# Reading the Toeplitz tiles of an S5 scan back in longer runs

## The chip, the core and the metric

The kernel runs on one core of a Trainium2 chip. The metric is the device time of one execution in microseconds (us). Three executions of the kernel before gave a median of 572.31 us (570.33 to 572.6).

A core has five engines with their own instruction streams: TensorE (PE, matrix products; PEld is its weight load), VectorE (DVE), ScalarE (ACT), GpSimd (POOL) and SyncE (SP), which here issues nearly all transfers (DMAs). Each engine works strictly in its own order. Between engines only semaphores order the work: an instruction names semaphores with a value, and it and everything behind it on its engine stand still until these are reached.

## The reference

One decoder layer on x (1024 tokens by 1024), then a final RMSNorm. Cut to what matters here:

```python
h = rms_norm(x, gain) * (1 + scl) + shift        # adaLN from cond = silu(c)
u, z_ssm, qd, kd, vd, z_diff, qs, ks, vs, z_swa = split_cols(h @ w_in)
y_ssm  = s5_mixer(u, ...)          * silu(z_ssm)   # 16 groups of 16 channels, 64 complex states each
y_diff = diff_attention(qd, kd, vd, ...) * silu(z_diff)            # 4 heads, full causal
y_swa  = sliding_window_attention(qs, ks, vs, ...) * silu(z_swa)   # 4 query heads, window 128
out = rms_norm(x + gate * (concat(y_ssm, y_diff, y_swa) @ w_out), final_gain)
```

Inside `s5_mixer` a diagonal complex recurrence runs over the 1024 tokens. Its output per group is y = Re(C s) + D u, then a GELU and a gated linear unit.

## The kernel before, in words

**The scan in blocks of eight.** The 1024 tokens are cut into 128 blocks of 8. Within a block the output of a group depends on the block's own eight inputs through a 128 by 128 lower block-Toeplitz matrix (8 by 8 lags of 16 by 16), and on the state that comes in from the blocks before. `ssm_lags` builds the lag matrices K (16 rows, per group 8 lags of 16 columns) with small products (`pK`), adds D at lag 0 on VectorE, writes K to the scratch `kscr[m]` in device memory (m is one of two halves of the 16 groups, 8 groups each; every group has 7 lags of zeros ahead of its 8 lags, 15 x 16 elements), and reads the Toeplitz matrix back: partition (s, h) of group a gets the 128 elements that begin s lags into that group's run. That is tile `T` (lines 664 to 684). `ssm_state(m)` makes the states (`pV` products, then `tg` and `Xs` on VectorE), `ssm_out(q)` for q = 0 to 3 does the products `pY` = T u + CA Xs into a bank of PSUM, the GELU in tile `gw`, and stores to the scratch `yscr` (lines 1104 to 1140). `ssm_glu` finishes later.

**Around it.** The S5 work stands between the projections, in this order on TensorE: the key tile `ks`, the query tiles `qs0` and `qs1` of the window attention (`p_ks`, `p_qs`), the gate `z0` (`p_z`), then values `v0` (`p_v`, 256 columns wide, weights in two halves), `q0`, `k0`. A projection's weights are loaded by SP (`wr_...`), split on ScalarE into a high part (`wh_...`) and on GpSimd or VectorE into a low part (`wl_...`), and multiplied with h (`hh`, `hl`) in three products. `next_w` (line 966) issues the load two projections ahead and the split one ahead. The results are copied out of PSUM by ScalarE and VectorE: `ev_q` (line 1174) writes `qs0m`, `qs1m` (two tiles each, both engines), `ev_silu` writes `z`, with a tanh on ScalarE and a product on VectorE.

**What sets the order.** A planner (`Model`, `Mixer`) with its own costs picks, while the program is written, which generator gets to add its next piece. The order on each engine is fixed after that.

**The pages.** Every large tile is one of 50 pages of 128 x 4096 bytes: `page()` (line 249) asks a pool with the one tag `pg` and `bufs=NPG`, where `NPG = 50` (line 240). All 50 are taken long before the S5 block, so a new tile takes over the page of an old one, and its first writer must wait for the last readers and writers of the old one. No line of the kernel says which old tile that is: the pool decides it while the program is built, in the order of the page() calls and of the releases. The planner does not know of it either.

**SP's semaphores.** SP's transfers use eight completion semaphores in turn. A transfer waits for the one eight before it.

**Names in the trace.** All operations have line L109, since one helper records them all, so tiles are told apart by name. The profile leaves out buffer numbers: `wl_v` is either half of the low part.

Of the kernel before, what the change touches and what calls it, by code (L numbers as in the profile page):

```python
# [24 lines left out]
def dap(t, offset, dims):  # L25
    return bass.AP(tensor=t.tensor, offset=t.offset + offset, ap=[list(d) for d in dims])
# [203 lines left out]
def body(ctx, tc, x, c, norm_gain, ada_w, ada_b, w_in, w_out, lam_re, lam_im, log_step,  # L230
# [13 lines left out]
    PE, SP = Eng(mdl, "PE", nc.tensor), Eng(mdl, "SP", nc.sync)  # L244
# [4 lines left out]
    def page(name, shape=(128, 1024), dt=F32):  # L249
        return big.tile(list(shape), dt, name=name, tag="pg", bufs=NPG)  # L250

    def pst(tag, name, shape=(128, 512)):
        t = psum.tile(list(shape), F32, name=name, tag=tag, bufs=BUFS[tag])
        mdl.slot(tag, BUFS[tag], t.tensor.name)
        if tag != "pp":
            held.add(t.tensor.name)
        return t

    def rel(*ts):

        for t in ts:
            held.discard(t.tensor.name)

    def bank(tag, n=1):

        def f():
            ring = mdl.ring.get(tag, [])
            if len(ring) + n <= BUFS[tag]:
                return 0.0
            olds = ring[:n - (BUFS[tag] - len(ring))]  # L270
            if any(o in held for o in olds):
                return 1e9
            return max(max(mdl.w.get(o, 0.0), mdl.r.get(o, 0.0)) for o in olds)
        return f

    def when(cond):
        return lambda: 0.0 if cond() else 1e9

    def tts(o, a, b, op, eng=None):
        (eng or V).tensor_tensor(o, a, b, op)  # L280
# [79 lines left out]
    X = []  # L360
# [67 lines left out]
    PW = {}  # L428
# [192 lines left out]
    kscr = [dram.tile([16, 8, 15, 16], F32, name=f"kscr{m}") for m in range(2)]  # L621

    def ssm_lags():
        kz = page("kz", (16, 8, 7, 16))
        G.memset(kz, 0.0)
        for m in range(2):
            SP.dma_start(kscr[m][:, :, 0:7, :], kz)
        yield (Cn, bank("pt"))
        psc = pst("pt", "psc", (128, 2, 128))
        for u in range(2):  # L630
            PE.transpose(psc[:, u], Cn[:, u], ident)
        A.activation(prm[:, 3], psc.rearrange("p a b -> p (a b)"), AF.Copy)
        rel(psc)
        AP = PW["AP"]

        CA = [[page(f"CA{m}{g2}", (128, 4, 9, 16)) for g2 in range(2)] for m in range(2)]
        PW["CA"] = CA
        u0, u1 = page("ca0", (128, 4, 9, 16)), page("ca1", (128, 4, 9, 16))
        v3 = lambda t, r: t[r].rearrange("p a b c -> p (a b c)")
        for m in range(2):  # L640
            yield ("V",)
            sl = slice(4 * m, 4 * m + 4)
            a4 = [AP[:, u, sl][:, :, :, None].to_broadcast([128, 4, 9, 16]) for u in range(2)]
            c4 = [CT[:, u, sl][:, :, None, :].to_broadcast([128, 4, 9, 16]) for u in range(2)]
            tts(u0, a4[0], c4[0], OP.mult)
            tts(u1, a4[1], c4[1], OP.mult)
            yield ("V",)
            for g2, r in enumerate(RH):
                tts(v3(CA[m][g2], RH[0]), v3(u0, r), v3(u1, r), OP.subtract)
            yield ("V",)  # L650
            tts(u0, a4[0], c4[1], OP.mult)
            tts(u1, a4[1], c4[0], OP.mult)
            yield ("V",)
            for g2, r in enumerate(RH):
                V.scalar_tensor_tensor(v3(CA[m][g2], RH[1]), v3(u0, r), -1.0, v3(u1, r),
                                       op0=OP.mult, op1=OP.subtract)

        yield (dn, bank("pt"))
        dT = cst.tile([16, 16], F32, name="dT")
        pd = pst("pt", "pd", (16, 16))  # L660
        PE.transpose(pd, dn, ident[:16, :16])
        A.activation(dT, pd, AF.Copy)
        rel(pd)
        Tm = [page(f"T{m}", (128, 8, 8, 16)) for m in range(2)]
        for m in range(2):
            K = page(f"K{m}", (16, 8, 8, 16))
            for g2 in range(2):
                yield (CA[m][g2], BS, bank("pt"))
                p = pst("pt", "pK", (16, 4, 128))
                for a in range(4):  # L670
                    PE.matmul(p[:, a], lhsT=BS[:, 4 * m + a, g2],
                              rhs=CA[m][g2][:, a, 0:8, :].rearrange("p a b -> p (a b)"), start=True, stop=True)
                A.activation(K.rearrange("p (a g) b c -> p g a (b c)", g=2)[:, g2], p, AF.Copy)
                rel(p)
            yield (K,)
            dd = sml.tile([16, 8, 16], F32, name="dd", bufs=1)
            tts(dd, ident[:16, None, :16].to_broadcast([16, 8, 16]),
                dT[:, 8 * m:8 * m + 8, None].to_broadcast([16, 8, 16]), OP.mult)
            tts(K[:, :, 0, :], K[:, :, 0, :], dd, OP.add)

            SP.dma_start(kscr[m][:, :, 7:15, :], K)
            SP.dma_start(Tm[m].rearrange("p a b c -> p a (b c)"),
                         dap(kscr[m], 0, [[16, 8], [15 * 128, 16], [15 * 16, 8], [1, 128]]))
        PW["T"] = Tm


# [345 lines left out]
    SM = {"st": 0, "y": 0}  # L1032
# [71 lines left out]
    def ssm_out(q):  # L1104

        m, g2 = divmod(q, 2)
        c0 = math.sqrt(2.0 / math.pi)
        yield (when(lambda: ("x", m) in SM and "T" in PW),)
        yield (SM["X"][m], PW["T"][m], bank("ps"))
        CA, Tm, Uu, Xs = PW["CA"], PW["T"], SM["U"], SM["X"][m]  # L1110
        p = pst("ps", "pY", (128, 4, 128))
        for a in range(4):
            pr = 4 * m + a
            g = 2 * pr + g2
            PE.matmul(p[:, a], lhsT=Tm[m][:, g % 8].rearrange("p a b -> p (a b)"), rhs=Uu[m][:, g % 8],
                      start=True, stop=False)
            PE.matmul(p[:, a], lhsT=CA[m][g2][:, a, 1:9, :].rearrange("p a b -> p (a b)"), rhs=Xs[:, g2, a],
                      start=False, stop=True)
        yield (p, "A")
        w = page("gw", (128, 2, 4, 128))  # L1120
        A.activation(w[:, 0], p, AF.Square)
        yield (w, "V")
        V.tensor_scalar(w[:, 0], w[:, 0], 0.044715, 1.0, op0=OP.mult, op1=OP.add)
        tts(w[:, 0], w[:, 0], p, OP.mult)
        yield (w, "A")
        A.activation(w[:, 0], w[:, 0], AF.Tanh, scale=c0)
        yield (w, "V")
        V.scalar_tensor_tensor(w[:, 1], w[:, 0], 1.0, p, op0=OP.add, op1=OP.mult)
        rel(p)
        for tt in range(8):  # L1130
            SP.dma_start(dap(yscr, (m * 8 + g2) * 16 * 1024 + tt * 128, [[1024, 16], [32 * 1024, 4], [1, 128]]),
                         w[tt * 16:(tt + 1) * 16, 1])
        SM["y"] += 1
        if SM["y"] == 4:
            GW = page("gw", (128, 2, 256))
            YG = [page(f"yg{f}", (128, 8, 128)) for f in range(2)]
            for f in range(2):
                SP.dma_start(GW[:, f], dap(glu_w, f * 128 * 256, [[256, 128], [1, 256]]))
                SP.dma_start(YG[f].rearrange("p a b -> p (a b)"), yscr[f * 128:(f + 1) * 128, :])
            PW["glu"] = (GW, YG)  # L1140
# [33 lines left out]
    def ev_q(name):  # L1174

        q = [page(f"{name}m{m}", dt=F32R) for m in range(2)]

        def f(p, n):
            cs_ = slice(n * 512, (n + 1) * 512)
            hi(q[0], R0, p, R0, cs_)  # L1180
            hi(q[1], R1, p, R1, cs_)
            lo(q[0], R1, p, R0, q[0], R0, cs_)
            lo(q[1], R0, p, R1, q[1], R1, cs_)
        return q, f

    def ev_k(name, m4=True):

        k = [page(f"{name}m{m}", dt=F32R) for m in range(4 if m4 else 3)]

        def f(p, n):  # L1190
            cs_ = slice(n * 512, (n + 1) * 512)
            hi(k[0], R0, p, R0, cs_)
            hi(k[1], R1, p, R1, cs_)
            lo(k[2], R0, p, R0, k[0], R0, cs_)
            lo(k[-1], R1, p, R1, k[1], R1, cs_)
            for m in range(4 if m4 else 2):
                src, dst = (R0, R1)[m % 2], (R1, R0)[m % 2]
                (acopy if name == "ks" else DUP[m])(k[m][dst, cs_], k[m][src, cs_])
        return k, f
# [318 lines left out]
    d_k, f = ev_k("ks")  # L1518
    proj(f)
    d_q = []  # L1520
    for a in range(2):
        q_, f = ev_q(f"qs{a}")
# [6 lines left out]
    for t in ORDER:  # L1529
# [6 lines left out]
        else:  # L1536
            z_ = page(t)
            f = ev_silu(z_)
# [82 lines left out]
    while live or opened < len(parts):  # L1621
# [7 lines left out]
        f, e = mix.first()  # L1629
# [3 lines left out]
        i, n, c, k = u  # L1633
# [35 lines left out]
```

## Time and profile before

| | |
|---|---|
| median of three runs | 572.31 us |
| the profiled execution: its own time | 574.51 us |
| its span, first to last instruction | 572.7 us |
| granted TensorE clock | 0.991 |
| busy: PE, DVE, ACT, POOL | 553.5, 407.0, 262.5, 188.2 us |
| the two reads of `T` | 512 KB each, issued at 135.80 and 143.52 us |
| packets of all transfers | 60634, 57.12 MB |

The profiled execution's own time is 1.8 us more than its span, and 2.2 us above the median of the runs. Times inside the span are given in us from its start. In the rows of a timeline the columns are start, duration, engine, line, operation, output tile <- input tiles, shapes and count of what was merged; in brackets stands how long the engine was idle before and which work ended that. A matmul's duration is modelled, and matmuls overlap: successive starts are 0.23 us apart for a 512-column product.

### The profile page before, as it was taken

The page shows a single profiled execution, that of the slowest core. Times are in us where ns is not written, and L with a number is a line of the kernel's source. Part 1 is how long each engine was busy: PE and PEld are TensorE (multiplying, and loading weights), DVE is VectorE, ACT ScalarE, POOL GpSimd, SP SyncE. Part 2 cuts the span into 40 slices and gives each one's busy share as a digit, 9 for nine tenths or more (in the row PEclk, how much of TensorE's full clock was granted, in tenths as well). Part 3 has the DMA queues.
Part 4 walks back from the last instruction along what each step waited for, and adds up shares of the span by engine and source line. Part 5 has one row for each costly group of instructions (what it writes and reads, how often), then busy time and mean ns, then how long its engine had stood idle before and what let it go on. Part 6 is the DMA issues. An engine that isn't in the chain of part 4 may idle for free.

```text
span 572.7 us, 9240 instructions
## 1 busy us (share of the span) xinstructions
PE 553.5 (97%) x3170; PEld 463.7 (81%) x3170; DVE 407.0 (71%) x1061; ACT 262.5 (46%) x595; POOL 188.2 (33%) x339
## 2 busy tenths in 40 slices
PE   8999999999997999999999999999999999799995
PEld 6667888888887996777788889998888888688884
DVE  3885996997687656778666777744877877666434
ACT  5445221255142545435555766535558545533111
POOL 3354270000135036442646172323332912210011
PEclk9999999999999999999999999999999999899998
DMA  8994076002711430437320111015025604014211
GB/s 287 354 351 94 3 187 153 0 2 47 148 37 47 77 117 38 178 127 226 106 73 2 38 37 38 2 37 158 28 83 170 189 1 129 1 74 147 94 38 73
DMA packets 60634, 57.12 MB, mean 100 GB/s; under 512 B 11375, under 2 KB 52906, under 8 KB 60586
## 3 DMA queue, kind: packets, MB, share of 16 engines
q1 hardware_dynamic: 60518, 56.50, 33.1%
q8 instruction: 25, 0.41, 0.3%
q14 instruction: 23, 0.19, 0.1%
q10 hardware_dynamic: 68, 0.02, 0.0%
HBM read 46.83 MB, written 9.68 MB: 99 GB/s over the span
## 4 chain that ended last, share of the span: by engine, by line
PE 76%; DVE 11%; DMA 5%; ACT 3%; issue 2%; POOL 1%; SPq 1%; POOLq 0%; DVEq 0%
PE po L109 13%; PE pb L109 8%; PE p_v L109 7%; PE p_k L109 6%; PE p_z L109 6%; PE pdO L109 6%; PE p_q L109 5%; PE pS L109 5%; PE p_zs L109 4%; DVE tg L109 3%; PE pdT L109 3%; DMA x<-in_x_dram 2%; PE p_vs L109 2%; PE p_zu L109 2%; PE pa L109 2%
## 5 line engine op out<-in xcount | busy, mean ns | idle before, releaser
L109 ACT ACTIVATE sp<-sp,dmx 128x128 f32<-128x128 f32 (+7 forms) x64 | 49.0, 768 | 16.5 <-DVE dmx L109 15.4
L109 PE MATMUL po<-woh,yh 128*128 128x512 f32 (+1 forms) x136 | 52.5, 386 | 1.1 <-ACT yh L109 1.1
L109 PE MATMUL po<-wol,yh 128*128 128x512 f32 (+1 forms) x136 | 51.6, 379 | 0.5 <-POOL wol L109 0.5
L109 PE MATMUL po<-woh,yl 128*128 128x512 f32 (+1 forms) x136 | 51.4, 378 | 0.0
L109 POOL TENSOR_SCALAR dmx<-dmx 128x1 f32<-128x1 f32 x32 | 8.2, 255 | 111.3 <-ACT oo L109 110.5
L109 DVE CUSTOM_DVE_ANT_0 sp<-pS,bd 128x384 f32<-128x384 f32 (+3 forms) x64 | 33.6, 552 | 10.7 <-PE pS L109 10.5
L109 PE MATMUL p_v<-wh_v,hh 128*128 128x256 f32 x128 | 37.8, 295 | 0.0
L109 PE MATMUL p_v<-wl_v,hh 128*128 128x256 f32 x128 | 36.4, 284 | 1.0 <-POOL wl_v L109 1.0
L109 PE MATMUL p_v<-wh_v,hl 128*128 128x256 f32 x128 | 36.2, 283 | 0.0
L109 POOL TENSOR_TENSOR swp<-swp,swm 128x256 f32<-128x256 f32 x30 | 20.4, 712 | 41.0 <-DVE swm L109 31.9
L109 ACT ACTIVATE jk<-res 128x512 f32<-128x512 f32 (+1 forms) x16 | 9.9, 616 | 46.5 <-DVE res L109 46.5
L109 PEld LDWEIGHTS po<-woh,yh 128*128 128x128 f32 x136 | 25.8, 189 | 5.9 <-ACT yh L109 1.5
L109 PEld LDWEIGHTS po<-wol,yh 128*128 128x128 f32 x136 | 25.8, 190 | 5.2 <-POOL wol L109 1.0
L109 PEld LDWEIGHTS po<-woh,yl 128*128 128x128 f32 x136 | 25.7, 189 | 4.8
L109 PE MATMUL p_k<-hh,wh_k 128*128 128x512 f32 x64 | 26.4, 413 | 0.0
L109 POOL TENSOR_TENSOR wl_z<-wr_z,wh_z 128x256 fp32r<-128x256 f32 x16 | 11.6, 755 | 44.5 <-ACT wh_z L109 44.5
L109 PE MATMUL p_q<-hh,wh_q 128*128 128x512 f32 x64 | 26.1, 407 | 0.0
L109 PEld LDWEIGHTS p_v<-wl_v,hh 128*128 128x128 f32 x128 | 24.4, 191 | 1.8 <-POOL wl_v L109 1.4
L109 PE MATMUL p_z<-hh,wh_z 128*128 128x512 f32 x64 | 25.7, 401 | 0.0
L109 PE MATMUL p_q<-hh,wl_q 128*128 128x512 f32 x64 | 25.2, 393 | 0.0
L109 PEld LDWEIGHTS p_v<-wh_v,hh 128*128 128x128 f32 x128 | 24.4, 191 | 0.9 <-issue 0.8
L109 PE MATMUL p_k<-hh,wl_k 128*128 128x512 f32 x64 | 25.1, 393 | 0.0
(486 smaller groups left out, 1674.1 us busy)
## 6 DMA issues: line engine op xcount, KB each, us to landing
aw<-in_ada_w_dram SPq DMA_DIRECT2D x32, 256.0 KB
x<-in_x_dram SPq DMA_DIRECT2D x8, 512.0 KB
gaw<-in_ada_w_dram SPq DMA_DIRECT2D x8, 512.0 KB
wo<-in_w_out_dram SPq DMA_DIRECT2D x8, 512.0 KB
xr<-in_x_dram SPq DMA_DIRECT2D x8, 512.0 KB
out_dram<-res SPq DMA_DIRECT2D x16, 256.0 KB
yt<-ycat SPq DMA_DIRECT2D x48, 64.0 KB
wr_z<-in_w_in_dram SPq DMA_DIRECT2D x4, 512.0 KB
```

The source lines that it names most:

```text
L109: return f(*args, **kw)
```

## The change

The read-back of T takes other tiles and other transfers. Before, one tile of 128 x (8 groups x 128) was filled by one transfer of 1024 runs (128 partitions x 8 groups) of 128 elements (512 bytes). Now each m has two tiles of 128 x 960, one for four groups each, and each is filled by one transfer of 128 runs of 848 elements (3392 bytes): from a partition's first lag in its first group to its last in the fourth, the 112 elements between two groups' matrices included. The product takes its 128 columns at a stride of 240. So a tile pair brings 868 KB in 256 runs where one brought 524 KB (512 x 1024 bytes) in 1024 runs.

```diff
-        Tm = [page(f"T{m}", (128, 8, 8, 16)) for m in range(2)]
+        Tm = [[page(f"T{m}{a}", (128, 960)) for a in range(2)] for m in range(2)]
...
             SP.dma_start(kscr[m][:, :, 7:15, :], K)
-            SP.dma_start(Tm[m].rearrange("p a b c -> p a (b c)"),
-                         dap(kscr[m], 0, [[16, 8], [15 * 128, 16], [15 * 16, 8], [1, 128]]))
+            for a in range(2):
+                SP.dma_start(Tm[m][a][:, 0:848], dap(kscr[m], a * 960, [[16, 8], [15 * 128, 16], [1, 848]]))
         PW["T"] = Tm
...
-        yield (SM["X"][m], PW["T"][m], bank("ps"))
+        yield (SM["X"][m], PW["T"][m][0], PW["T"][m][1], bank("ps"))
...
-            PE.matmul(p[:, a], lhsT=Tm[m][:, g % 8].rearrange("p a b -> p (a b)"), rhs=Uu[m][:, g % 8],
+            PE.matmul(p[:, a], lhsT=Tm[m][g % 8 // 4][:, g % 4 * 240:g % 4 * 240 + 128], rhs=Uu[m][:, g % 8],
                       start=True, stop=False)
```

The order of the work on PE, DVE, ACT and POOL is the same in both programs, instruction for instruction; SP has the two added transfers. What differs besides is who takes over whose page, since T now takes four pages and not two. From the addresses in the two built programs, for the tiles that the next 50 us write:

| new tile | takes the page of, before | takes the page of, now |
|---|---|---|
| second tile of `qs0m` (`qs0m1`) | `wl_ks` | `wh_qs` of qs0 |
| `wh_z` (z0's weights, high part) | `wh_qs` of qs0 | the first `tg` of state m = 0 |
| `qs1m`, first tile (`qs1m0`) | `wr_z` | `wr_z` |
| `wh_v`, second half (`wh_v01`) | `wl_qs` of qs1 | `jm` (a table for the window masks) |
| `wl_v`, second half (`wl_v01`) | `jm` | `wr_v`, first half |
| `z` of z0 | `wr_v`, first half | `wr_v`, second half |

The program's waits show it. ScalarE, in the place where it copies the queries out and splits the weights of z0, before (the names end in the tile's index and a running number; p_qs00 is qs0's first 512 tokens, p_qs01 its second; in brackets the semaphores waited for):

```order
L109 ACTIVATE qs0m0_1515<-p_qs00_1523 64x512 [waits PE_49]
L109 ACTIVATE qs0m1_1516<-p_qs00_1523 64x512
L109 ACTIVATE qs0m0_1515<-p_qs01_1552 64x512 [waits PE_49]
L109 ACTIVATE qs0m1_1516<-p_qs01_1552 64x512
L109 ACTIVATE wh_z0_1593<-wr_z0_1517 128x1024 [waits DMAHW5_49]
L109 ACTIVATE qs1m0_1587<-p_qs10_1600 64x512 [waits PE_49,Activation_49,Pool_49]
```

And now:

```order
L109 ACTIVATE qs0m0_1519<-p_qs00_1527 64x512 [waits DMAHW4_49,PE_49]
L109 ACTIVATE qs0m1_1520<-p_qs00_1527 64x512 [waits PE_49]
L109 ACTIVATE qs0m0_1519<-p_qs01_1556 64x512 [waits PE_49]
L109 ACTIVATE qs0m1_1520<-p_qs01_1556 64x512
L109 ACTIVATE wh_z0_1597<-wr_z0_1521 128x1024 [waits DMAHW7_49,DVE_49]
L109 ACTIVATE qs1m0_1591<-p_qs10_1604 64x512 [waits PE_49,DMAHW1_49,Activation_49,Pool_49]
```

The second row has a wait that was not there. The value that it asks of TensorE's semaphore is raised by the 47th of the 48 products of `p_qs` for qs0, the last to read `wh_qs`. The DMAHW4 of the first row is the write of the second K to scratch. `wh_z` now also waits for VectorE, for the last `Xs` of state m = 0.

ScalarE again, some 20 us later, at the split of the weights of v0 and the tanh of z0; before:

```order
L109 ACTIVATE wh_v00_1710<-wr_v0_1589 128x1024 [waits DMAHW6_49]
L109 ACTIVATE wh_v01_1717<-wr_v0_1590 128x1024 [waits DMAHW7_49,DMAHW1_49]
L109 ACTIVATE z0_1707<-p_z00_1724 128x512 [waits PE_49,DMAHW3_49,Activation_49,Pool_49]
L109 ACTIVATE z0_1707<-p_z01_1751 128x512 [waits PE_49]
L109 ACTIVATE wh_q0_1784<-wr_q0_1708 128x1024 [waits DMAHW0_49,DVE_49]
```

And now:

```order
L109 ACTIVATE wh_v00_1714<-wr_v0_1593 128x1024 [waits DMAHW0_49]
L109 ACTIVATE wh_v01_1721<-wr_v0_1594 128x1024 [waits DMAHW1_49,DMAHW3_49,DVE_49,Pool_49]
L109 ACTIVATE z0_1711<-p_z00_1728 128x512 [waits PE_49,Activation_49,Pool_49]
L109 ACTIVATE z0_1711<-p_z01_1755 128x512 [waits PE_49]
L109 ACTIVATE wh_q0_1788<-wr_q0_1712 128x1024 [waits DMAHW2_49,DVE_49]
```

The second half of `wh_v` now waits for VectorE: for the last of the four `bsw`, which read `jm`. The first `z` waits for GpSimd in both, but before for the last `wl_v` of the first half, and now for the last `wl_v` of the second. `wh_q` waits for the last pair of `tg` on VectorE in both (before for its first, now for its second).

SP at the transfers in question, before:

```order
L109 DMA T0_1419<-kscr0_151 128x8x128 [waits DMAHW5_49,DMAHW3_49,DMAHW6_49,DMAHW2_49,DMAHW1_49]
L109 DMA kscr1_152<-K1_1473 128x1x128 [waits DVE_49]
L109 DMA T1_1420<-kscr1_152 128x8x128 [waits DMAHW4_49,DMAHW3_49,PE_49]
L109 DMA wr_z0_1517<-in_w_in_dram 128x8x128 [waits PE_49]
L109 DMA wr_v0_1589<-in_w_in_dram 128x4x256
```

And now:

```order
L109 DMA T00_1419<-kscr0_151 128x1x848 [waits DMAHW5_49,DMAHW3_49,DMAHW6_49,DMAHW2_49,DMAHW1_49]
L109 DMA T01_1420<-kscr0_151 128x1x848
L109 DMA kscr1_152<-K1_1476 128x1x128 [waits DMAHW4_49,DVE_49]
L109 DMA T10_1421<-kscr1_152 128x1x848 [waits DMAHW4_49,PE_49]
L109 DMA T11_1422<-kscr1_152 128x1x848 [waits PE_49]
L109 DMA wr_z0_1521<-in_w_in_dram 128x8x128 [waits DMAHW7_49]
L109 DMA wr_v0_1593<-in_w_in_dram 128x4x256 [waits DMAHW0_49,PE_49]
```

The second K's write stands one transfer later, and `wr_z` two. The PE semaphores of the second T pair are raised by early products (`pV`, `pK`); that of `wr_v` by the last `p_qs` of qs0.

## The prediction

> **What bounds the kernel now.** First the page's head and its chain of work that ended last, then the waits of TensorE between 130 and 240 us (us in total, times, longest), the stretch in which T is read and used:
>
> ```profile
> span 572.7 us, 9240 instructions
> PE 76%; DVE 11%; DMA 5%; ACT 3%; issue 2%; POOL 1%; SPq 1%; POOLq 0%; DVEq 0%
> ```
>
> ```profile
> PE pY L109 <- DVE gw L109: 2.4, 1, 2.4
> PE p_v L109 <- POOL wl_v L109: 1.0, 2, 0.5
> PE psw L109 <- DVE swm L109: 0.2, 1, 0.2
> ```
>
> TensorE sets the end: its order is fixed, and every us that it stands still is added to the time. In this stretch it stands for 3.4 us (2.4 and 1.0) that better supply could give back. The chain's 11% of DVE and 5% of DMA lie largely here, so I read the timelines of the others. SP, then ScalarE:
>
> ```profile
> 135.80 0.62 SPq L109 DMA_DIRECT2D T<-kscr  x1
> 137.15 0.96 SPq L109 DMA_DIRECT2D kscr<-K  x1
> 143.52 0.62 SPq L109 DMA_DIRECT2D T<-kscr  x1
> 144.19 1.58 SPq L109 DMA_DIRECT2D wr_z<-in_w_in_dram  x1
> ```
>
> ```profile
> 142.45 1.20 ACT L109 ACTIVATE qs0m<-p_qs 64x512 fp32r<-64x512 f32 x2 [0.53 <-PE p_qs L109]
> 147.89 1.20 ACT L109 ACTIVATE qs0m<-p_qs 64x512 fp32r<-64x512 f32 x2 [4.24 <-PE p_qs L109]
> 154.09 1.06 ACT L109 ACTIVATE wh_z<-wr_z 128x1024 fp32r<-128x1024 f32 x1 [4.99 <-DMA wr_z<-in_w_in_dram]
> 158.11 1.21 ACT L109 ACTIVATE qs1m<-p_qs 64x512 fp32r<-64x512 f32 x2 [2.96 <-POOL wl_z L109]
> 162.36 1.20 ACT L109 ACTIVATE qs1m<-p_qs 64x512 fp32r<-64x512 f32 x2 [1.93 <-PE p_qs L109]
> 163.59 2.01 ACT L109 ACTIVATE wh_v<-wr_v 128x1024 fp32r<-128x1024 f32 x2
> 168.94 0.60 ACT L109 ACTIVATE z<-p_z 128x512 f32<-128x512 f32 x1 [3.34 <-POOL wl_v L109]
> ```
>
> The second K's write, issued at 137.15 behind the first T, lets the second T go only at 143.52. Behind it wr_z lands as ScalarE's wait ends (154.09). Wh_z, wl_z and qs1m follow, and VectorE is late:
>
> ```profile
> 143.69 1.39 DVE L109 TENSOR_TENSOR qs0m<-p_qs,qs0m 64x512 fp32r<-64x512 f32 x2 [0.50 <-ACT qs0m L109]
> 145.11 1.29 DVE L109 TENSOR_TENSOR tg<-tg,PH 128x508 f32<-128x508 f32 x2
> 150.55 1.38 DVE L109 TENSOR_TENSOR Xs<-tg,tg 64x508 f32<-64x508 f32 x2
> 151.96 1.29 DVE L109 TENSOR_TENSOR tg<-pV,PH 128x512 f32<-128x512 f32 x2
> 159.41 1.41 DVE L109 TENSOR_TENSOR qs1m<-p_qs,qs1m 64x512 fp32r<-64x512 f32 x2 [6.16 <-ACT qs1m L109]
> 164.85 2.31 DVE L109 TENSOR_TENSOR tg<-tg,PH 128x508 f32<-128x508 f32 x2
> 171.28 1.43 DVE L109 SCALAR_TENSOR_TENSOR bsw<-jm 128x256 f32<-128x256 f32 x4
> 172.74 0.69 DVE L109 SCALAR_TENSOR_TENSOR z<-z,p_z 128x512 f32<-128x512 f32 x1
> 173.35 2.02 DVE L109 TENSOR_TENSOR tg<-tg,PH 128x508 f32<-128x508 f32 x2
> 175.40 2.22 DVE L109 TENSOR_TENSOR Xs<-tg,tg 64x508 f32<-64x508 f32 x2
> 178.24 0.97 DVE L109 TENSOR_SCALAR gw<-gw 128x512 f32<-128x512 f32 x1
> 179.85 0.93 DVE L109 TENSOR_SCALAR gw<-gw 128x512 f32<-128x512 f32 x1
> 181.41 1.47 DVE L109 SCALAR_TENSOR_TENSOR gw<-gw,pY 128x512 f32<-128x512 f32 x2
> ```
>
> From 159.41 to the first gw product that frees a bank for pY (the first of the pair at 181.41) VectorE works without a pause, and TensorE waits for it:
>
> ```profile
> 147.24 0.39 PE L109 MATMUL p_qs<-hl,wh_qs 128*128 128x512 f32 x1
> 153.82 0.38 PE L109 MATMUL pY<-U,T 128*128 128x128 f32 x2
> 182.15 0.49 PE L109 MATMUL pY<-U,T 128*128 128x128 f32 x2 [2.36 <-DVE gw L109]
> ```
>
> So up to 3.4 us hang on when wr_z lands. That is what a faster T could give.
>
> **The change, part by part.** *The reads of T.* The profile has no run of 3392 bytes. What it has is the windows with T alone in flight (140 to 142 us), and one of the wr_vs and wr_ks loads, also in 512-byte runs (last two columns: DMA share, GB/s):
>
> ```profile
> 87.00:88.00 1.00, 1.00 (x6) 0.84 (x5) 0.00 (x0) 0.38 (x1) 0.00 (x0) 1.00 1.17 336
> 140.00:141.00 1.00, 1.00 (x6) 0.84 (x5) 0.00 (x0) 0.95 (x3) 0.00 (x0) 1.00 0.64 105
> 141.00:142.00 1.00, 1.00 (x6) 0.84 (x5) 0.04 (x1) 0.93 (x1) 0.00 (x0) 1.00 0.64 103
> ```
>
> T runs at 104 GB/s with half of the engine share, so 524 KB take 5.0 us. The 868 KB take 2.6 us at 336 GB/s and 8.3 us at 104: -2.4 to +3.3 us for each m. The half share with one queue full says that half of the engines work, and these would then give 168 GB/s at the other loads' rate: 5.2 us. That is nearest, so I take no change in T's own time. The Trainium skill's page "DMA: Bandwidth & Descriptors" (section "Why a DMA increments its semaphore by 16 and not by 1") says that a transfer uses the largest number of engines up to 16 that divides both sides' slowest dimension; T's source has 8 there before and after, the trace's 0.64 against 1.17 agrees, and by it longer runs would win no engines.
>
> *The added issues.* Two more at about 0.66 us. The first ends at 137.1, as the second K's write is issued. The second delays wr_z's issue by 0.7 us, but wr_z is behind T in the queue anyway.
>
> *The first page.* The second qs0m copy now waits for the 47th p_qs of qs0, the row at 147.24, which ends at 147.6. It took place at 143.05 (second of the pair at 142.45); now it is done at 147.7 + 0.6 = 148.3. VectorE's qs0m, which follows it in the same order, moves from 143.69 to 148.3, so +4.6 us. Behind it stand, without a gap, all of VectorE's work up to 153.25 (151.96 + 1.29), 9.56 us: it ends at 157.9. The last piece reads the bank that the first pY needs. TensorE came to pY at 153.82 and now stands there until 157.9: **4.1 us** of stop.
>
> *wh_z* waits for the Xs that ended at 151.93 and now ends at 156.5. That is after 154.1, when wr_z is there: T has 2.4 us of cover. Then 1.06 us of wh_z, 2.80 of wl_z, 1.21 of qs1m: VectorE's qs1m starts at 161.8 and not at 159.41, **+2.4 us** (its 6.16 us of idle take up the rest). GpSimd's rows:
>
> ```profile
> 155.28 2.80 POOL L109 TENSOR_TENSOR wl_z<-wr_z,wh_z 128x256 fp32r<-128x256 f32 x4 [34.57 <-ACT wh_z L109]
> 164.73 4.17 POOL L109 TENSOR_TENSOR wl_v<-wr_v,wh_v 128x256 fp32r<-128x256 f32 x4 [6.36 <-ACT wh_v L109]
> 172.94 4.14 POOL L109 TENSOR_TENSOR wl_v<-wr_v,wh_v 128x256 fp32r<-128x256 f32 x4 [4.04 <-DVE bsw L109]
> ```
>
> The same four pieces take 2.80 us beside an idle VectorE and 4.15 beside a busy one, and VectorE's tg pair takes 2.31 beside GpSimd and 1.29 without: the two slow each other. TensorE's last p_qs moves by 4.1, so wh_v comes at about 167.5 and wl_v's first half from 168.6; the tg pair is then clear of it, and of the 13.3 us from 159.41 to the end of bsw (172.71) 1.0 falls away. bsw ends at 161.8 + 12.3 = 174.1 (175.1 if nothing falls away).
>
> *The second page and z.* The second wh_v waits for that, 1.05 us: 175.2 (before 165.6). Then wl_v's second half, 2.80 to 4.14: 178.0 to 180.3 with both ends of bsw. The tanh of z waits for it, 0.60, since z's page was the second wr_v: VectorE's z starts at 178.7 to 181.0 and not at 172.74. VectorE stands still meanwhile, with all of tg, Xs and gw behind it. From z to the first freed bank were 9.4 us (172.74 to 182.10). With tg and Xs at 1.29 and 1.38 (GpSimd has nothing then, as wl_q needs wh_q, which needs this tg) they are 7.8; with the two gw steps of 0.95 at half too, 6.8. So pY goes on between 178.7 + 6.8 = 185.5 and 181.0 + 9.4 = 190.4, against 182.15: +3.3 to +8.2 us. I take wl_v at 2.80, since VectorE is idle beside it, and 7.8, as wl_q runs beside the gw steps: 178.7 + 7.8 + 0.1 = 186.6, **+4.5 us**; as some pieces will be slowed that I count as clear, I go to **+4.9**. TensorE's own work from the first pY to the second is 182.15 - 153.82 - 3.4 = 24.9 us, from 157.9 to 182.8: it waits about 4 us there, and the 1.0 us for wl_v is gone. Behind this pY the order is the same and TensorE is the bound, so the end moves by the same.
>
> **Sum.** 574.5 + 4.9 = 579.4 us for an execution like the profiled one. That lies 2.2 above the median of the runs, so I forecast 572.3 + 4.9 = 577.2.
>
> **Rivals.** *The reads decide (the other side).* The place is wr_z's landing: if T takes 2.6 us and the page waits are met by then, wr_z lands 4.8 us earlier, and the 3.4 us of stops go: 568.9. For it speaks that the chain before runs over just this transfer; against it that the 47th p_qs cannot end before 147.6 whatever the transfers do, and wh_z not before Xs. From the moment that the first page's wait costs over 2 us this is decided.
>
> *The second stop hides.* If VectorE and GpSimd slow each other much less than I count, or VectorE makes up more in its idle time, pY's second stop ends with TensorE's own work at 182.8 or little later, +0.7 to +2.8: 573.0 to 575.1, which is no difference that can be measured.
>
> *The reads are slower.* If the rate stays 104 GB/s for the longer runs, T takes 8.3 us: the second K and the second T are each 3.3 late, wr_z 6.6; 2.4 are covered, and 4.2 come on top: 581.4. For it speaks that T's rate is so far below the other loads'; against, that nothing but its eight-fold outer dimension and its overlapping sources explains it, and these allow 168.
>
> **How the numbers follow.** The two pages as worked out: 0.72, with 575.5 to 580.5 as its own range. The second stop hides: 0.12. The reads are slower: 0.09. The reads decide: 0.07. The range for 8 in 10 is 573.8 to 581.0. About 0.5% (2.9 us) is what a measurement of this kernel can tell from no change. Slower by more (above 575.2) is most of the first case and the third, 0.82; within it 0.12, faster 0.06.
>
> **What would show it.** In the profile of the changed kernel: the second qs0m copy at 147.7 with a wait for PE; TensorE idle for some 4 us before the first pY, ended by VectorE's tg, and again before the one near 187, ended by gw; no wait of p_v for wl_v; ScalarE's two wh_v apart, the second after bsw; VectorE idle for about 4 us before qs1m and again before z. T's own transfers should not stand in the chain. I am wrong if pY starts at 153.8, or if z follows bsw on VectorE without a pause; and right for a wrong reason if wh_z's wait ends with wr_z's landing and not with Xs.

## The result, and the profile after

The changed kernel takes 579.71 us (median of four executions, 577.52 to 581.26) against 571.66 us for the kernel before in the same comparison: a ratio of 1.0135 (95% interval 1.0111 to 1.0159), or 6.3 to 9.1 us more. The forecast was 577.2 with a range of 573.8 to 581.0, slower with a chance of 0.82. Direction and range held; the centre was 2.5 us low, and one of the steps to it was wrong.

The profiled execution after took 577.52 us, the fastest of the four. The head of its page, then the waits of TensorE between 130 and 240 us (us in total, times, longest):

```profile
span 575.7 us, 9237 instructions
```

```profile
PE pY L109 <- DVE gw L109: 4.7, 1, 4.7
PE pY L109 <- DVE tg L109: 3.3, 1, 3.3
```

Before, TensorE stood for 2.4 us (gw) and 1.0 us (wl_v) here. Now it stands for 3.3 us ahead of the first pY, which waits for a tg, and for 4.7 us ahead of the second, which waits for gw. No p_v waits for wl_v any more. Both stops are the ones that were forecast (4.1 and about 4). The first pY is the place where the products with m = 0 start, near 154 us before; the second is where those with m = 1 start, near 182. (Two of the expectations below call this one the third pY.)

The timelines of the same stretch: SP, ScalarE, VectorE, TensorE.

```profile
135.03 1.25 SPq L109 DMA_DIRECT2D T<-kscr  x2
136.39 0.59 SPq L109 DMA_DIRECT2D kscr<-K  x1
144.44 1.19 SPq L109 DMA_DIRECT2D T<-kscr  x2
145.68 0.45 SPq L109 DMA_DIRECT2D wr_z<-in_w_in_dram  x1
```

```profile
144.46 0.59 ACT L109 ACTIVATE qs0m<-p_qs 64x512 fp32r<-64x512 f32 x1 [3.31 <-DMA kscr<-K]
146.88 1.82 ACT L109 ACTIVATE qs0m<-p_qs 64x512 fp32r<-64x512 f32 x3 [1.83 <-PE p_qs L109]
157.46 1.06 ACT L109 ACTIVATE wh_z<-wr_z 128x1024 fp32r<-128x1024 f32 x1 [8.76 <-DMA wr_z<-in_w_in_dram]
175.05 1.06 ACT L109 ACTIVATE wh_v<-wr_v 128x1024 fp32r<-128x1024 f32 x1 [6.20 <-issue]
179.09 1.09 ACT L109 ACTIVATE z<-p_z 128x512 f32<-128x512 f32 x2 [2.99 <-POOL wl_v L109]
```

```profile
147.51 1.41 DVE L109 TENSOR_TENSOR qs0m<-p_qs,qs0m 64x512 fp32r<-64x512 f32 x2 [5.10 <-ACT qs0m L109]
154.38 1.38 DVE L109 TENSOR_TENSOR Xs<-tg,tg 64x508 f32<-64x508 f32 x2
155.79 1.29 DVE L109 TENSOR_TENSOR tg<-pV,PH 128x512 f32<-128x512 f32 x2
162.72 1.41 DVE L109 TENSOR_TENSOR qs1m<-p_qs,qs1m 64x512 fp32r<-64x512 f32 x2 [5.64 <-ACT qs1m L109]
173.53 1.43 DVE L109 SCALAR_TENSOR_TENSOR bsw<-jm 128x256 f32<-128x256 f32 x4
179.73 0.69 DVE L109 SCALAR_TENSOR_TENSOR z<-z,p_z 128x512 f32<-128x512 f32 x1 [4.76 <-ACT z L109]
```

```profile
156.54 0.79 PE L109 MATMUL pY<-U,T 128*128 128x128 f32 x2 [3.35 <-DVE tg L109]
187.09 0.80 PE L109 MATMUL pY<-U,T 128*128 128x128 f32 x2 [4.66 <-DVE gw L109]
```

The second K's write goes out at 136.39 here and at 137.15 in the profile before, so 0.76 us has to be added to these times to set them beside the old ones. Done so, the page waits stand near where the prediction put them. The second qs0m copy comes with the 47th p_qs, and VectorE's qs0m at 148.3 (forecast 148.3). Xs ends at 156.5 (forecast 156.5). bsw ends at 175.7 (forecast 174.1 to 175.1), and the second half of wh_v starts 0.1 us after it and not behind the first half; its row names only "issue", but by the program's order it waits for the last bsw. VectorE stands still for 4.76 us until z, at 180.5 (forecast 178.7 to 181.0). The second pY starts at 187.85, 5.7 us later than before (forecast 4.9).

Behind it the two profiles come nearer to each other. On their own scales the second pY lies 4.9 us apart, but the two executions only 3.0 us (577.52 and 574.51). About 1.6 us come back near 494 us, where the profile before runs at half clock (a granted TensorE clock of 0.5) behind a stop of 2.6 us, and this one does not. So in this pair the end did not move by what the second pY moved, though the prediction let both move alike, and the size of the loss is read from the ratio of the runs.

One row does not fit: wh_z's wait of 8.76 us ends with the landing of wr_z, at 158.2 on the old scale, and not with Xs at 156.5. T's reads were to have 2.4 us of cover, and were over it by 1.7 us. So what share do the pages have, and what share the reads?

### The profile page after: what moved, and what is told of

The parts are those of the page before. It is cut to its first block, busy times and chain, and to the rows that moved or that the text cites. A ratio compares the mean times of both kernels' runs of the same rounds, so it can differ in the third digit from the quotient of the medians.

```text
span 575.7 us, 9237 instructions
## 1 busy us (share of the span) xinstructions
PE 552.5 (96%) x3170; PEld 462.9 (80%) x3170; DVE 403.9 (70%) x1061; ACT 262.6 (46%) x595; POOL 187.4 (33%) x339
## 4 chain that ended last, share of the span: by engine, by line
PE 57%; DVE 6%; ACT 2%; issue 1%; POOL 1%; POOLq 0%; DVEq 0%; ACTq 0%
PE po L109 13%; PE p_v L109 7%; PE p_k L109 7%; PE p_z L109 6%; PE pdO L109 5%; PE p_q L109 5%; PE pS L109 5%; PE pdT L109 3%; PE pwO L109 1%; PE pG L109 1%; DVE sp L109 1%; PE psw L109 1%; PE pwT L109 1%; PE pY L109 1%; POOL wol L109 1%
## 5 line engine op out<-in xcount | busy, mean ns | idle before, releaser
L109 PE MATMUL p_q<-hl,wh_q 128*128 128x512 f32 x64 | 25.1, 393 | 0.0
```

Source lines behind the costliest of these rows:

```text
L109: return f(*args, **kw)
```

## The experiments

Each run was compared with executions of the kernel before on the same chip; e1 to e4 share one set of these (median 572.56 us), e5 to e8 another (573.03), e9 and e10 a third (573.58). All have the same order of instructions as the kernel before on TensorE, VectorE and ScalarE, but for what their diff adds. "Ratio" is to the kernel before.

### The pages without the reads, and the reads without the pages

**e1_pages**: two idle pages beside the old T.

```diff
-        Tm = [page(f"T{m}", (128, 8, 8, 16)) for m in range(2)]
+        Tm, Dm = [], []
+        for m in range(2):
+            Tm.append(page(f"T{m}", (128, 8, 8, 16)))
+            Dm.append(page(f"D{m}", (128, 960)))
...
+            nc.gpsimd.memset(Dm[m][:, 0:1], 0.0)
...
+        if g2:
+            nc.gpsimd.memset(PW["D"][m][:, 1:2], 0.0)
```

> The kernel before with its own two transfers of T (512-byte runs), and two idle pages, D0 and D1, taken beside T0 and T1 and held as long. So 50 pages must do with two fewer, and nothing else changes. The takeovers that follow: wh_z takes the first tg of state m = 0, the second half of wh_v takes jm, z takes the second half of wr_v, as in the change; only the second qs0m tile takes a harmless page (the weights wr_qs, whose last reader on VectorE ends at 143.2), so this is the second page wait without the first. Pages theory: wh_z stays at 154.1 and bsw at 172.7, wh_v's second half follows bsw, wl_v's second half ends at 176.7 to 178, z on VectorE starts at 177.4 to 178.7 instead of 172.74, and the second pY starts 2.2 to 6 us later than 182.15: 3.5 us over the kernel before, about 575.5. Reads theory (only T's longer transfers cost): no difference, 572.

Measured: 576.21 us, ratio 1.0067 (1.0045 to 1.0089), so +3.8 us for two pages that hold nothing. ScalarE, VectorE and the waits of TensorE:

```profile
171.07 1.06 ACT L109 ACTIVATE wh_v<-wr_v 128x1024 fp32r<-128x1024 f32 x1 [7.21 <-issue]
175.12 1.09 ACT L109 ACTIVATE z<-p_z 128x512 f32<-128x512 f32 x2 [2.98 <-POOL wl_v L109]
```

```profile
169.56 1.43 DVE L109 SCALAR_TENSOR_TENSOR bsw<-jm 128x256 f32<-128x256 f32 x4
175.75 0.69 DVE L109 SCALAR_TENSOR_TENSOR z<-z,p_z 128x512 f32<-128x512 f32 x1 [4.76 <-ACT z L109]
```

```profile
PE pY L109 <- DVE gw L109: 5.3, 1, 5.3
```

The second page wait stands here without the first, and with no reads changed. (ScalarE also waits 1.53 us and not 0.53 ahead of its first qs0m copy, for the second K's write; TensorE does not stand for that.) Behind bsw come wh_v (1.06 us), four pieces of wl_v (2.82) and the tanh of z (0.60), and with the handoffs VectorE stands for the same 4.76 us as in the change.

**e2_reads**: the change's four pages and transfers, and two pages freed elsewhere.

```diff
-        CA = [[page(f"CA{m}{g2}", (128, 4, 9, 16)) for g2 in range(2)] for m in range(2)]
+        CA = [[page(f"CA{m}0", (128, 4, 9, 16))] * 2 for m in range(2)]
```

> The change with all its transfers, and two pages freed elsewhere: each pair of CA tiles shares one page. The second of a pair overwrites the first, so this kernel computes the scan's output with one half of CA for both; the instructions and their order stay. With that no page wait of the change is left: qs0m, wh_z, wh_v and z take pages as harmless as before. Pages theory, with no change in T's own time: 572.3 within 1 us, stops as before. Reads theory: T's pairs still take 1.7 to 2.4 us longer each than before's single transfers, wr_z lands 3 to 4 us later than 154.06, and since all of VectorE's work hangs on it, the second pY starts 3 to 4 us later: 575.5 to 576.5, with no stop before the first pY.

Measured: 575.94 us, ratio 1.0054 (1.0036 to 1.0073), +3.1 us. SP's second T, ScalarE's wh_z, and the waits of TensorE:

```profile
143.52 1.24 SPq L109 DMA_DIRECT2D T<-kscr  x2
```

```profile
155.68 1.06 ACT L109 ACTIVATE wh_z<-wr_z 128x1024 fp32r<-128x1024 f32 x1 [7.93 <-DMA wr_z<-in_w_in_dram]
```

```profile
PE p_v L109 <- POOL wl_v L109: 1.9, 3, 0.9
PE p_v L109 <- ACT z L109: 0.7, 1, 0.7
PE pY L109 <- DVE gw L109: 0.4, 1, 0.4
```

The page waits are gone, and the loss is not. From the second T's issue to wh_z it is 12.2 us and not 10.6 as before: the reads alone cost, which the forecast had at nothing. The expectation had the loss as one longer stop ahead of the second pY, and that is not how it came. In this profile (574.32 us, below the median) the stops are short ones ahead of p_v, and with 3.0 us no longer in sum than the 3.4 us before. What is longer is the time at half clock, which the window shows (busy, PEclk, DMA share, GB/s):

```profile
177.00:184.00 7.00, 6.00 (x25) 0.52 0.25 75
```

The kernel before has half of that, 3.4 us from 183.5 on. Set beside each other by the second K's write (issued at 135.90 here, at 137.15 before), TensorE is 1.3 us later than before when it is through the second pY. So the profile shows 1.3 of the 3.1 us; where the others of the median lie it does not show.

### Why the reads are slow

**e3_reads16**: as e2_reads, with the two outer dimensions of T's source exchanged.

```diff
-dap(kscr[m], a * 960, [[16, 8], [15 * 128, 16], [1, 848]])
+dap(kscr[m], a * 960, [[15 * 128, 16], [16, 8], [1, 848]])
```

> As the run with the two pages freed elsewhere, and T's source dimensions swapped: 16 rows h outside, 8 lags s inside, so that the slowest dimension is 16 and not 8. T's partitions are thus in another order than U's, and the scan's output is that of permuted lags; bytes and runs are the same. If the number of engines follows that dimension, the DMA share with T alone in flight rises from 0.64 to near 1.2 and each pair of 868 KB takes 3 to 4.5 us in place of 7 to 8; wr_z then lands before 151 and the 3.4 us of stops of the kernel before go: 567 to 569.5. If T is bound by something else (its overlapping source rows, the write side), the share stays at 0.64 and the time is that of the run with 8: no gain against it.

Measured: 566.38 us, ratio 0.9900 (0.9880 to 0.9921). The windows with T in flight (last two columns: DMA share, GB/s), of the change and then of this run, and this run's transfers and wh_z:

```profile
140.00:141.00 1.00, 1.00 (x6) 0.83 (x5) 0.00 (x0) 0.97 (x2) 0.00 (x0) 1.00 0.48 112
141.00:142.00 1.00, 1.00 (x6) 0.82 (x5) 0.82 (x1) 0.15 (x1) 0.00 (x0) 1.00 0.52 126
```

```profile
137.00:138.00 1.00, 1.00 (x7) 0.81 (x6) 0.39 (x1) 0.97 (x2) 0.00 (x0) 1.00 1.03 302
139.00:140.00 1.00, 1.00 (x6) 0.84 (x5) 0.02 (x1) 0.98 (x2) 0.00 (x0) 1.00 1.01 249
```

```profile
135.24 1.18 SPq L109 DMA_DIRECT2D T<-kscr  x2
141.27 1.16 SPq L109 DMA_DIRECT2D T<-kscr  x2
```

```profile
149.03 1.06 ACT L109 ACTIVATE wh_z<-wr_z 128x1024 fp32r<-128x1024 f32 x1 [0.58 <-DMA wr_z<-in_w_in_dram]
```

The same bytes in the same runs move at 249 to 302 GB/s in these windows (204 in the one between them) instead of 112 to 126, and the DMA share doubles. e2_reads, which differs only in that 8 stands outside and not 16, has 119 to 136 GB/s in its windows from 140 to 142 us. The rule on the number of engines that the prediction quoted from the Trainium skill ("DMA: Bandwidth & Descriptors", section "Why a DMA increments its semaphore by 16 and not by 1") is thereby tested with 8 and with 16, and these traces agree. From the first T's issue to the second's, which waits for the second K's write behind it, it takes 6.0 us here (135.24 to 141.27), 7.7 us before and 9.4 us in the change. With wr_z there at 149.0, TensorE has no stop over 0.2 us in the whole stretch.

**e5_pages16**: the change with all four pages, and only this exchange.

> The change with its four pages as they are (all page waits), and only T's source dimensions swapped, 16 rows h outside, so that T runs on 16 engines (T's partitions are in another order than U's, and the scan's output is that of permuted lags). This is the case of the prediction: both page waits, and no longer read. Pages theory: wr_z lands near 149, the second qs0m copy still waits for the 47th p_qs, wh_z starts when Xs ends (about 156), the first pY stands for 3 to 4 us and the second for about 4: 576 to 577.5, some 4 to 5 over the kernel before and 2 to 3 under the change, whose wr_z comes later still. Reads theory (page waits bind only because the reads are late): 566.5 to 569, as with fast reads and freed pages.

Measured: 578.18 us, ratio 1.0075 (1.0049 to 1.0101), +4.3 us. ScalarE's wh_z, and TensorE's waits:

```profile
155.71 1.06 ACT L109 ACTIVATE wh_z<-wr_z 128x1024 fp32r<-128x1024 f32 x1 [7.09 <-DVE Xs L109]
```

```profile
PE pY L109 <- DVE tg L109: 3.3, 1, 3.3
PE pY L109 <- DVE gw L109: 3.0, 1, 3.0
```

This is the case that the prediction described: wh_z's wait ends with Xs, and the reads cost nothing. Its +4.3 us (2.8 to 5.8) agree with the forecast of 4.9. In its profile the second pY starts at 185.62, or 186.47 on the old scale (the second K's write goes out at 136.30), 4.3 us later than before. That the fast reads gain 5.7 us with harmless pages and lose 4.3 with the change's shows the page waits as a cause of their own. The first wait adds little to the second: e1_pages, without it, lost 3.8 us, and the intervals overlap (though e1_pages has the old reads and this run the fast ones). A stop ahead of the first pY is time that TensorE doesn't spend standing ahead of the second.

### Moving the second T

**e4_late**: the kernel before, with the read of the second T issued behind wr_z and wr_v.

```diff
-            SP.dma_start(Tm[m].rearrange("p a b c -> p a (b c)"), ...)
+            if m:
+                PW["late"] = lambda: nc.sync.dma_start(to(1), src(1))
+                SP.dma_start.account(to(1), src(1))
+            else:
+                SP.dma_start(to(0), src(0))
...
             load_w(*tiles[i + 2])
+            if tiles[i + 2][0] == "v0":
+                PW["late"]()
```

(`account` books the transfer in the planner at its old place, so that the planner's order stays.)

> The kernel before, with one transfer moved: the read of the second T is issued behind wr_z and the two wr_v, not ahead of them (it is needed only by the third pY, at 182). Theory that the stops of the kernel before hang on wr_z's landing: wr_z is issued at 138 and lands by 148, wh_z follows qs0m at 148 to 149.5 instead of 154.09, VectorE's qs1m comes some 5 us earlier, and both stops (2.4 and 1.0 us) go: 568 to 569. Rival, that VectorE's own amount of work sets the second pY: at most 1 us is gained, 571.

Measured: 567.33 us, ratio 0.9911 (0.9890 to 0.9932), 5.1 us faster than the kernel before. SP, ScalarE, VectorE:

```profile
136.89 0.53 SPq L109 DMA_DIRECT2D wr_z<-in_w_in_dram  x1
144.08 0.64 SPq L685 DMA_DIRECT2D T<-kscr  x1
```

```profile
148.20 1.06 ACT L109 ACTIVATE wh_z<-wr_z 128x1024 fp32r<-128x1024 f32 x1
```

```profile
154.44 1.41 DVE L109 TENSOR_TENSOR qs1m<-p_qs,qs1m 64x512 fp32r<-64x512 f32 x2 [1.31 <-ACT qs1m L109]
175.68 1.47 DVE L109 SCALAR_TENSOR_TENSOR gw<-gw,pY 128x512 f32<-128x512 f32 x2
```

wr_z was stuck behind a transfer that waits for the landing of K and that nobody needs for another 30 us. With wr_z moved past it wh_z has no wait left, it starts 5 us earlier and VectorE's qs1m 4 us earlier (this profile's second K's write goes out at 136.22, so 0.93 us is added to its times), and both stops of the kernel before are gone.

**e6_late_long**: the same with the change's long runs; the second pair takes its pages and goes out behind wr_q, so that at the peak two pages fewer are in use.

```diff
-        Tm = [[page(f"T{m}{a}", (128, 960)) for a in range(2)] for m in range(2)]
+        Tm = [[page(f"T0{a}", (128, 960)) for a in range(2)], None]
...
+            def late():
+                Tm[1] = [page(f"T1{a}", (128, 960)) for a in range(2)]
+                for a in range(2):
+                    nc.sync.dma_start(Tm[1][a][:, 0:848], src(1, a))
```

> The change with the second pair of T moved: its two pages are taken and its two transfers issued behind the load of wr_q (needed only by the third pY). At the peak there are two pages fewer in use, qs0m and wh_z take harmless pages as before, and wr_z goes out behind the second K's write without waiting for it; only the wait of wh_v's second half for bsw is left of the page waits. If a page wait costs only where the engine behind it is already late: wr_z lands by 150, VectorE is 5 us ahead, bsw ends at 168, wh_v and wl_v follow in time, and nothing stands: 567 to 569, as with the second T moved in the kernel before. If the wait for bsw costs its 3 to 4 us wherever it stands: 570.5 to 572.

Measured: 573.18 us, ratio 0.9992 (0.9975 to 1.0010). My favoured reading, that the wait for bsw costs only where VectorE is late already, falls: against e4_late this kernel has only the one page wait (and long runs that nothing waits for), and it is 4.6 us slower by the two ratios. VectorE, and TensorE's wait, and below them the second pY of e4_late:

```profile
174.07 0.69 DVE L109 SCALAR_TENSOR_TENSOR z<-z,p_z 128x512 f32<-128x512 f32 x1 [4.76 <-ACT z L109]
181.09 1.47 DVE L109 SCALAR_TENSOR_TENSOR gw<-gw,pY 128x512 f32<-128x512 f32 x2
```

```profile
PE pY L109 <- DVE gw L109: 3.0, 1, 3.0
```

```profile
177.16 0.39 PE L109 MATMUL pY<-U,T 128*128 128x128 f32 x2
```

The 4.76 us are a round trip that starts from VectorE itself (bsw, then ScalarE, GpSimd, ScalarE, then z), so an earlier VectorE only starts it earlier. In e4_late the first gw product ends at 176.4 (175.68 and half of the pair's 1.47) and the second pY starts at 177.16: VectorE has 0.8 us in hand there, not 4.76. The stop that remains, 3.0 us, and the half clock behind it (3.4 us long) account for about the 4.6 us.

**e7_one_page**: half of the change, the first T in two tiles, the second as before.

```diff
-        Tm = [[page(f"T{m}{a}", (128, 960)) for a in range(2)] for m in range(2)]
+        Tm = [[page(f"T{m}{a}", (128, 960)) for a in range(2)] if m == 0 else [page(f"T{m}", (128, 8, 8, 16))] * 2
+              for m in range(2)]
```

> Half of the change: the first T in two tiles of long runs, the second T as before in one tile of 512-byte runs; three pages and not four. Of the page waits one small one is left (the second qs0m tile takes the second K's page, and waits for the landing of its write, about 1.5 to 2 us). Theory that both the pages and the reads of the change cost: here only one longer read, T's first pair about 1.5 us longer, so that the second K, the second T and wr_z are that much later: 573.5 to 574.5. Rival, that any page more brings the waits of the change: 576 to 577.

Measured: 573.71 us, ratio 1.0014 (0.9994 to 1.0035). TensorE's waits:

```profile
PE pY L109 <- DVE gw L109: 2.4, 1, 2.4
PE pY L109 <- DVE tg L109: 1.1, 1, 1.1
```

The small wait that was expected is there: ScalarE's second qs0m copy waits 2.35 us for the second K's write, and the 1.1 us ahead of the first pY follow from it. The ratio cannot be told from no change, so whether the one longer read costs anything here is not shown. But the rival falls: with one page more the other tiles still get pages whose last users are long done (wh_z takes wl_qs, the second half of wh_v takes wl_qs of qs1), and only the second page more brings the waits of the change. In this kernel it is a step and not a price per page.

### The clock after a stop

**e8_change** is the change once more, **e9_busy** the change with idle products in its two stops.

```diff
+        if g2 == 0:
+            fill = psum.tile([128, 512], F32, name="fill", tag="pt", bufs=BUFS["pt"])
+            for i in range((12, 16)[m]):
+                nc.tensor.matmul(fill, lhsT=HH[0][:, 0:128], rhs=HH[0][:, 0:512], start=True, stop=True)
         p = pst("ps", "pY", (128, 4, 128))
```

> The change itself again, beside the others on one chip, for the sum: 579 to 580.5; two stops of 3 to 5 us before the first and the second pY, each followed by a stretch of half clock. If the extra over the two stops comes from such stretches, the executions spread over 2 to 4 us, and the slower ones show a granted clock lower by 0.003 for each 1.7 us.

> The change, with products on TensorE whose results nobody reads put into the two stops: 12 of 512 columns (0.23 us each, 2.8 us) ahead of the first pY, 16 (3.7 us) ahead of the second. Nothing else moves. Theory that each stop costs a stretch of half clock besides its own length (1.3 us after the first, 1.0 to 2.8 after the second): both pY start when VectorE lets them, as in the change, and then run at full clock; 576.5 to 578.5 against 579.8, and no PEclk of 0.5 between 150 and 195. Rival, that the granted clock falls for another reason (heat, or the time in the kernel): half clock at the same places, and 579 to 581.

Measured: e8_change 579.84 us, ratio 1.0115 (1.0090 to 1.0139); e9_busy 578.58 us, ratio 1.0094 (1.0078 to 1.0110). The executions of e8_change spread over 4 us, as expected, but four of the five show the same clock, 0.988, at 578.02 to 580.18 us, so the clock does not tell the slower ones from the faster, against the expectation. In its profile the stops are 3.3 and 2.8 us, and the first is followed by 6.8 us of half clock. The windows of TensorE (busy, PEclk, DMA share, GB/s), of the change as first profiled and then of e9_busy:

```profile
156.00:158.00 2.00, 1.46 (x7) 0.50 0.83 245
187.00:189.00 2.00, 1.91 (x9) 0.50 0.24 41
```

```profile
156.00:158.00 2.00, 2.00 (x18) 1.00 0.74 233
187.00:189.00 2.00, 1.53 (x13) 1.00 0.16 27
```

After each stop the change runs at half clock, and with the stops filled it does not. The first pY shows the price: its products start 0.43 us apart and not 0.22, and TensorE, 3.5 us later than before at the first of them, is 4.9 us later after eleven. But it did not hold that nothing else moves: with the first pY through earlier, GpSimd's wl_v meets VectorE's tg pair, which takes 2.29 us and not 1.26, and the second pY starts 0.9 us later than in the change (187.47, or 188.79 on the old scale). The two ratios, 1.0115 and 1.0094, have intervals that overlap, so neither the gain nor its size is shown in the change. In the kernel before, the gain is clear of the noise.

**e10_before_busy** puts 8 such products ahead of the second pY of the kernel before:

> The kernel before with 8 such products (1.8 us) in its stop of 2.4 us ahead of the second pY. By the theory of the stops the half clock at 183.5, which takes about 1 us, is gone: 571.5 to 572.5 against 572.8. By the rival no change, or later by what the products delay pY (under 0.5 us).

Measured: 572.01 us, ratio 0.9971 (0.9956 to 0.9987), 0.7 to 2.5 us gained by products that nobody reads. The window 185 to 187 us of the kernel before, and below it that of this run, show what is taken away:

```profile
185.00:187.00 2.00, 2.00 (x11) 0.52 0.21 35
185.00:187.00 2.00, 2.00 (x21) 1.00 0.20 34
```

On the scale of the profile before (0.82 us taken off, as the second K's write goes out at 137.97), the second pY starts 0.35 us later than before, and TensorE is 1.3 us earlier when it is through.

## Why the prediction was right, and where it was wrong

- **The first page.** Right in place and nearly in size: VectorE's qs0m at 148.3 as forecast, a stop of 3.3 us and not 4.1. Its step "The last piece reads the bank that the first pY needs" was wrong; pY starts at 156.54, before the second piece of the tg pair can be done (155.79 + 1.29 = 157.1), so the first piece frees the bank; with half of the pair's 1.29 us taken off, the sum gives 3.4.
- **wh_z.** Wrong, in the way that the prediction named as right for a wrong reason: its wait ended with wr_z, not with Xs. The step that failed is "T's own time", taken as 5.2 us for 868 KB at 168 GB/s. Half of the engines was right; that they would reach half of the other loads' rate was not: 112 to 126 GB/s, or 6.9 to 7.8 us, which is 8 to 21% more than the 104 GB/s of the short runs. With 16 engines, too, T stayed below the 336 GB/s of those loads (201 to 302 GB/s in the windows from 137 to 140 us of e3_reads16 and e5_pages16); why is not shown. The rival "the reads are slower" (0.09) thus had the right mechanism and was given too little. By e2_reads it costs 3.1 us by itself; beside the page waits, which cover part of it, it adds 1.0115 less 1.0075, about 2.3 us (0.3 to 4.3, if the two intervals are taken as independent).
- **The second page and z.** Right: VectorE's idle time before z was 4.74 to 4.76 us (4.6 forecast) in the profile of every kernel that had this wait, and e1_pages shows the loss with no reads changed. In the change z came 1.8 us later than the 178.7 of the sum, nearly all of it wr_z's 1.7, and from z to the second pY it took 7.4 us and not 7.8.
- **The sum.** The forecast of 4.9 us was one for the page waits alone, and e5_pages16, which has them alone, measured 4.3 (2.8 to 5.8). The change measured 7.7 by its first comparison and 6.6 by its second. The difference is the reads; so the direction was not luck, since the page waits alone make the kernel slower. Besides, the sum lacked a term altogether, the half clock behind a stop: the kernel before has one such stretch in this part of the program, the profiled change two, and the prediction let the end move with the second pY, which the stretch near 494 us undoes in the profiled pair. How much of the total that is was not resolved; e9_busy puts it at 1.2 us with intervals that overlap.
- **The rivals.** "The reads decide", a gain, did not come about, but the place that it named was right: with fast reads and free pages the kernel gained 5.7 us. Its figure of 3.4 was too small; it had the stops and not the half clock behind them. "The second stop hides" is refuted by the stop of 4.7 us.

## What to carry to other kernels

When tiles share a pool that is full, two tiles more can change what later tiles wait for, and the diff doesn't show it: list which old tile each new one takes over, and look at who reads that one last and when. A wait that goes around through other engines and back to the same one starts when that engine gets there, so being earlier did not hide it here (4.76 us, against 0.8 in hand); look at how much that engine has in hand ahead of the bound. The longer runs helped T's rate little while its outer dimension kept half of the DMA engines out (112 to 126 GB/s where it had been 104), and the order of the dimensions helped it much; so order the dimensions first, and before that ask whether the transfer must stand ahead of the one that others wait for.

## What the runs showed of the hardware

- **Engines of a transfer.** With T's reads in flight, an outer source dimension of 8 gave a DMA share of 0.47 to 0.56 and 112 to 136 GB/s for runs of 3392 bytes (140 to 142 us of the change and of e2_reads), one of 16 a share of 0.87 to 1.04 and 201 to 302 GB/s (137 to 140 us of e3_reads16 and e5_pages16), with the same bytes.
- **Half clock after short stops.** A stop of 2.4 us in the kernel before was enough for a stretch of half clock, and one of 0.5 us (e10_before_busy) was not. The trace's clock record has these stretches at 3.4 or 6.8 us, and they start on a fixed grid: 183.5 and 494.1 us in the profile before lie 91.0 times 3.413 us apart. Laying that grid over the twelve profiles of this study, and leaving out the last 20 us of each, TensorE had stood idle for 0.57 to 1.00 of the 3.4 us ahead of 17 of the 18 stretches (0.50 ahead of the other), and for 0.56 at most where full clock went on. So it is less the length of one stop that decides than how much of a cell of the grid stands idle, and the same stop (2.6 us, near 494) brought half clock in the profile before and none in that of the change. The Trainium skill ("TensorE: Matmul & The Clock Gate", section "What's actually happening") has the free-running window of 3413 ns, and this trace agrees; it has the clock fall after a whole idle window, and here a little more than half of one was enough. Why five of the stretches last for two cells, though TensorE stood idle for only 0.11 to 0.64 of the first of the two, is not shown.
